# FoX attention of a hybrid decoder layer: plain fp32 on array tiles, 32x32 transposes on VectorE

## The chip, the cores and the metric

The kernel runs on one core of a Trainium2 chip. The metric is the device time of one execution in microseconds. The engines are named as in the profile: PE is TensorE's matrix multiplication (PEld its weight loads), DVE is VectorE, ACT is ScalarE, POOL is GpSimd, SP is SyncE, which issues most DMAs.

## The reference

One decoder layer on 1024 tokens of width 1024. All products are of float32. `u = rmsnorm(x)` is projected by `w_in` into 8 groups of 1024 columns and the forget gates; HGRN2 heads take four groups, FoX heads (16 of width 64) the other four. Their outputs, gated by SiLU, go through one output projection, are added to `x`, gated again and normalised. What the change touches is the FoX branch:

```python
log_f = log_sigmoid(fz + fb)
F = cumsum(log_f, axis=1).transpose(0, 2, 1)
for blk in range(S // Q):            # blocks of 128 queries
    logits = einsum('bhtd,bhsd->bhts', qb, kb) * scale + F[:, :, q0:q1, None] - F[:, :, None, :q1]
    probs = softmax(where(causal, logits, -inf), axis=-1)
    outs.append(einsum('bhts,bhsd->bhtd', probs, vb))
```

## The kernel before

Four stages follow each other: the norm of the input, eight HGRN heads, 16 FoX heads in eight pairs (a pair fills 128 partitions with two heads of 64), and the output projection with gate and norm.

Dense projections are made from two float32r parts of each operand (hi is the rounded value, lo the rest) in three matmuls, hi x hi, hi x lo and lo x hi, all on the full 128x128 array with 512 moving columns. They are jobs of a class `Ahead`: while a head's own steps wait for each other, `ahead.fill(columns)` issues about so many moving columns of the next projections (`FOX_FILL` holds the numbers), `ahead.until(mark)` issues jobs until a projection is done, and `ahead.flush()` issues small transposes that were put off. The numbers and the order of the jobs set the order on PE; the other engines follow the order in which a scheduler lists the instructions of the program. All rows of L363 are dense projections inside `Ahead`; each 512-token half of a job writes one of two PSUM buffers `ps` with 24 matmuls and is then read by ACT and DVE.

A FoX head is worked in two chunks of 512 queries (c = 1 first, then c = 0), and `Chunk.mix(following)` interleaves the values of one chunk with the logits and softmax of the next:

- `fox_q`, `fox_k`, `fox_v` read the projections out of PSUM: q and k become float32r parts (`kh`, `kl`; q holds hi in one half of the partitions and lo in the other, POOL copies k to both halves), v is turned to token-major by PE transposes (L485) and split (`vs`).
- `Chunk.softmax(b)`, for each of four blocks of 128 queries: logits as two float32r matmuls per piece of up to 512 keys (L816, L817); DVE adds the key bias and takes the minimum of the negated logits in one instruction (L820), the block's own keys with a causal bias that POOL has added (`fm`, L801); small DVE minima join the pieces (L826); ACT takes exp with the row sum (L827).
- `Chunk.transposed(j)`: PE transposes the probabilities of key block j, 128x128 each (L835), ACT and DVE split them into float32r parts (L844, L845; L838, L839 for the last block).
- `Chunk.mix`: two matmuls per key block add the values (L867, L868) in one PSUM buffer `po`; ACT and DVE add the two halves into the output (L873, L874).
- `norms` makes 1/Z of a head, through DRAM to all partitions; `finish` multiplies the output with 1/Z and with the gate on POOL and stores it.

The bias rows F come from DRAM (`fd`), one load of 512 KB a head (`biases`).

## Time and profile before

| what | value |
|---|---|
| median of 3 runs | 1362.05 us (1361.67 to 1363.15) |
| span of the profiled execution | 1361.6 us, mean granted PE clock 0.993 |
| PE busy | 1324.1 us, 97% of the span, 8756 matmul records |
| DVE, ACT, POOL busy | 802.6, 552.6, 373.7 us |
| first logits to last values of FoX | 549.7 to 1081.9 us |
| DMA | 100.93 MB, mean 74 GB/s |

The profiled execution's span is within 0.5 us of the median of the runs. A busy share counts from an instruction's start to its modelled end; consecutive matmuls overlap, so the pace of PE is read from the starts. Rows of groups give line, engine, operation, output <- inputs, shape and count, then busy time and the mean of one in ns, then the idle time of the engine ahead of them and what ended it. Matmul rows name the used part of the array (128*128, 128*32) and the moving operand. A plain float32 matmul appears as two records.

### The profile page before, as it was taken

How to read it: one execution, taken by the hardware profiler on the slowest of the kernel's cores; microseconds unless marked ns; L12 is line 12 of the kernel's file. 1: busy time of each engine (PE TensorE's matmuls, PEld its weight loads, DVE VectorE, ACT ScalarE, POOL GpSimd, SP SyncE). 2: the span in 40 equal slices, each digit the busy share in tenths (PEclk: the TensorE clock that was granted, in tenths of full speed). 3: DMA queues.
4: the chain of work that ended last, by engine and by line, in shares of the span. 5: the costliest groups of instructions: out<-in, count | busy, mean ns of one | idle time of the engine just before them, and what ended most of it. 6: DMA issues, size and time to landing. Idle time of an engine off the chain costs nothing.

```text
span 1361.6 us, 22260 instructions
## 1 busy us (share of the span) xinstructions
PE 1324.1 (97%) x8756; PEld 1116.9 (82%) x8756; DVE 802.6 (59%) x1976; ACT 552.6 (41%) x1128; POOL 373.7 (27%) x352
## 2 busy tenths in 40 slices
PE   6899999999999999999999999999999999999996
PEld 4787888888888878888888888888888888888895
DVE  6746575656746576576566666666666843333465
ACT  5413122221312233565555555555565711222455
POOL 3613123112211122344333333333342210101232
PEclk9999999999999999999999999999999999999998
DMA  7411111101101012112121112111123163212312
GB/s 282 144 45 63 48 38 58 63 17 63 48 32 63 19 47 80 47 56 70 55 71 55 56 55 70 54 55 55 70 84 118 63 240 108 85 47 70 132 63 78
DMA packets 35080, 100.93 MB, mean 74 GB/s; under 512 B 5008, under 2 KB 7312, under 8 KB 34976
## 3 DMA queue, kind: packets, MB, share of 16 engines
q1 hardware_dynamic: 34832, 98.99, 20.8%
q8 instruction: 69, 1.13, 0.3%
q0 software_dynamic: 144, 0.52, 0.1%
q14 instruction: 35, 0.29, 0.1%
HBM read 82.59 MB, written 16.91 MB: 73 GB/s over the span
## 4 chain that ended last, share of the span: by engine, by line
PE 87%; DVE 7%; ACT 4%; issue 1%; DMA 1%; SPq 0%; POOL 0%; DVEq 0%; ACTq 0%; POOLq 0%
PE ps L363 47%; PE pt L835 5%; PE ps L105 5%; PE ps L103 5%; PE ps L104 4%; PE po L868 3%; PE po L867 3%; PE lg L816 2%; PE lg L817 2%; PE ps L569 1%; PE gps L105 1%; PE gps L104 1%; PE gps L103 1%; DVE x L279 1%; PE po L712 1%
## 5 line engine op out<-in xcount | busy, mean ns | idle before, releaser
L363 PE MATMUL ps<-uhi,whi 128*128 128x512 f32 x896 | 355.9, 397 | 0.3 <-DVE q L451 0.3
L363 PE MATMUL ps<-ulo,whi 128*128 128x512 f32 x896 | 355.5, 397 | 0.0
L363 PE MATMUL ps<-uhi,wlo 128*128 128x512 f32 x896 | 354.6, 396 | 0.0
L88 POOL TENSOR_TENSOR wlo<-wf,whi 128x1024 fp32r<-128x1024 f32 x59 | 145.3, 2463 | 377.4 <-ACT whi L87 370.8
L363 PEld LDWEIGHTS ps<-uhi,whi 128*128 128x128 f32 x896 | 168.4, 188 | 31.5 <-PE ps L363 0.7
L363 PEld LDWEIGHTS ps<-ulo,whi 128*128 128x128 f32 x896 | 168.5, 188 | 30.4
L363 PEld LDWEIGHTS ps<-uhi,wlo 128*128 128x128 f32 x896 | 168.5, 188 | 30.4
L87 ACT CAST whi<-wf 128x1024 fp32r<-128x1024 f32 (+1 forms) x77 | 79.8, 1038 | 168.7 <-PE ps L104 90.4
L827 ACT ACTIVATE pr<-pr,mx 128x1024 f32<-128x1024 f32 (+7 forms) x128 | 99.6, 778 | 101.3 <-DVE mx L826 94.8
L845 DVE TENSOR_TENSOR pl<-pt,ph 128x512 fp32r<-128x512 f32 (+2 forms) x160 | 94.7, 607 | 75.9 <-ACT ph L844 74.6
L801 POOL TENSOR_TENSOR fm<-fbc,cst 128x128 f32<-128x128 f32 x128 | 59.0, 462 | 251.1 <-DVE mx L826 129.4
L844 ACT CAST ph<-pt 128x512 fp32r<-128x512 f32 (+2 forms) x160 | 79.8, 520 | 70.7 <-PE pt L835 60.1
L105 PE MATMUL ps<-yhi,wlo 128*128 128x512 f32 x256 | 99.6, 389 | 0.0
L103 PE MATMUL ps<-yhi,whi 128*128 128x512 f32 x256 | 99.6, 389 | 0.0
L104 PE MATMUL ps<-ylo,whi 128*128 128x512 f32 x256 | 99.6, 389 | 0.0
L820 DVE CUSTOM_DVE_ANT_0 pr<-lg,fbc 128x512 f32<-128x512 f32 (+3 forms) x176 | 82.0, 490 | 15.5 <-PE lg L817 15.2
L835 PE MATMUL pt<-cst,pr 128*128 128x128 f32 x576 | 89.3, 272 | 1.1 <-ACT pr L827 0.9
L835 PEld LDWEIGHTS pt<-cst,pr 128*128 128x128 f32 x576 | 71.4, 140 | 19.6 <-ACT pr L827 2.2
L816 PE MATMUL lg<-kh,q 128*128 128x512 f32 x192 | 74.7, 389 | 0.0
L817 PE MATMUL lg<-kl,q 128*128 128x512 f32 x192 | 64.1, 341 | 0.0
L867 PE MATMUL po<-ph,vs 128*128 128x512 f32 (+2 forms) x160 | 57.8, 361 | 0.1
L868 PE MATMUL po<-pl,vs 128*128 128x512 f32 (+2 forms) x160 | 57.9, 362 | 0.0
(214 smaller groups left out, 2498.3 us busy)
## 6 DMA issues: line engine op xcount, KB each, us to landing
wf<-in_w_in_dram SPq DMA_DIRECT2D x64, 512.0 KB
fbc<-fd SPq DMA_DIRECT2D x16, 512.0 KB
yf<-yd SPq DMA_DIRECT2D x16, 512.0 KB
wf<-in_w_out_dram SPq DMA_DIRECT2D x16, 512.0 KB
x<-in_xT_dram SPq DMA_DIRECT2D x8, 512.0 KB
pled<-pleo SPq DMA_DIRECT2D x16, 256.0 KB
xr<-in_xT_dram SPq DMA_DIRECT2D x16, 256.0 KB
yd<-sg SPq DMA_DIRECT2D x8, 512.0 KB
```

Of the source, the lines that this page charges most:

```text
L88: pin(lo_engine.tensor_tensor(out=lo, in0=src, in1=hi, op=ALU.subtract))
L103: pin(mm(ps, whi, uhi, start=i == 0, stop=False))
L104: pin(mm(ps, whi, ulo, start=False, stop=False))
L105: pin(mm(ps, wlo, uhi, start=False, stop=i == n - 1))
L363: pe(mm(ps, x, y, start=i == j == 0, stop=i == n - 1 and j == 2))
L816: pe(mm(ps[:, :w], tq, kh[:, s0 : s0 + w], start=True, stop=False))
L817: pe(mm(ps[:, :w], tq, kl[:, s0 : s0 + w], start=False, stop=True))
L827: nc.scalar.activation(pr, pr, AF.Exp, bias=mx[:, 0:1], scale=-1.0, accum_out=zs[:, b : b + 1])
L835: pe(nc.tensor.transpose(pt[:, b * P : (b + 1) * P], self.probs[b][:, j * P : (j + 1) * P], ident))
L845: nc.vector.tensor_tensor(out=pl, in0=pt[:, c0:], in1=ph, op=ALU.subtract)
L867: pe(mm(po[:, c0:], vs[:, j], ph, start=j == 0, stop=False))
L868: pe(mm(po[:, c0:], vs[:, j], pl, start=False, stop=j == nj - 1))
```

## The change

FoX is computed in plain float32 instead of float32r parts, on parts of the array.

- The keys are cut into groups of 32, and groups with an even and with an odd number are kept apart. A row of 128 partitions now holds 64 queries twice: four strips of 32 partitions, two strips of queries by two parities of key groups. `logits(b)` computes two such rows m = 2b + 1 and 2b, each of 64 queries against m + 1 groups of each parity: eight matmuls on array tiles of 64x32 (two row halves, four column strips), N = 32(m + 1) moving columns, into a pair of PSUM banks (L804). q and k are therefore held on both partition halves.
- DVE adds bias and takes the minimum for each m (L816), after POOL has added the causal bias to the last group of the row (`own`, L789; each `own(m - 2)` follows the reading of row m, which uses the same bias tile). `softmax()` of a whole chunk then joins the minima of the two parities (L828, L829), and for each m ACT takes exp with the sum (L836) and DVE transposes all 32x32 blocks of the row (L837) into `probs`. No split follows.
- `values()` multiplies on 64x64 tiles (L848): 64 keys of a group pair in a row half, even and odd pairs in the two column halves, 4 matmuls of up to 256 columns each for two pairs. They are all issued together, after the logits of the following chunk.
- The PSUM pools become two logits buffers of two banks and one buffer `po` of two banks, which the small transposes share. The projections of the next pair come in the order v, q, k, gate. `FOX_FILL` holds one number per pair, used twice a chunk.
- F is stored to DRAM by parity in two DMAs, and its rows come back in four loads a head. The loads of the HGRN outputs for the output projection go into other buffers that are free at that time.

The core of the diff:

```diff
-FOX_FILL = (
-    (1660, 3670, 8820, 2130, 2400),
...
+FOX_FILL = (9200, 12300, 12300, 12300, 12300, 12300, 9200, 4000)
...
-    causal = np.where(r[None, :] > r[:, None], np.float32(BIG), np.float32(0.0)).astype(np.float32)
+    query, key = 32 * (r // 64) + r % 32, 32 * (r // 32 % 2)
+    causal = np.where(key[:, None] + np.arange(32)[None, :] > query[:, None], np.float32(BIG), np.float32(0.0)).astype(np.float32)
...
-    fd = dram.tile([16, S], F32, name="fd")
+    fd = dram.tile([16, 2, CH], F32, name="fd")
...
-            tiles += [T_FQ + p + 1, T_FK + p + 1] + ([T_FG + p] if 0 < p < PAIRS_F - 2 else []) + [T_FV + p + 1]
+            tiles += [T_FV + p + 1, T_FQ + p + 1, T_FK + p + 1] + ([T_FG + p] if 0 < p < PAIRS_F - 2 else [])
...
     def fox_q(p):
-        q = q_t[p] = [fi.tile([P, S], F32R, name="q", tag="q", bufs=4) for _ in range(2)]
+        q = q_t[p] = [fi.tile([P, CH], F32, name="q", tag="q", bufs=4) for _ in range(2)]
...
     def fox_k(p):
-        kh = kh_t[p] = [fp.tile([P, S], F32R, name="kh", tag="kh", bufs=3) for _ in range(2)]
+        k = k_t[p] = [fp.tile([P, S], F32, name="k", tag="k", bufs=3) for _ in range(2)]
...
-                nc.scalar.copy(kh[i][hi, sl], ps[hi])
-                nc.vector.tensor_tensor(out=kl[i][hi, sl], in0=ps[hi], in1=kh[i][hi, sl], op=ALU.subtract)
-                for kk in (kh, kl):
-                    nc.gpsimd.tensor_scalar(
-                        out=kk[i][lo, sl], in0=kk[i][hi, sl], scalar1=1.0, scalar2=1.0, op0=ALU.mult, op1=ALU.mult
-                    )
+                nc.scalar.copy(k[i][half[0], sl], ps[half[i]])
+                nc.vector.tensor_copy(out=k[i][half[1], sl], in_=ps[half[i]])
...
-        vs = v_t[p] = [fp.tile([P, FB, P], F32R, name="vs", tag="vs", bufs=3) for _ in range(2)]
+        v = v_t[p] = fp.tile([P, 2 * FB, P], F32, name="v")
...
-                    nc.scalar.copy(dst[:, :, hi], pv[:, :, hi])
-                    nc.vector.tensor_tensor(out=dst[:, :, lo], in0=pv[:, :, hi], in1=dst[:, :, hi], op=ALU.subtract)
+                    pe(nc.tensor.transpose(pt[:, 0, b * P : (b + 1) * P], vt[:, b * P : (b + 1) * P], ident))
+                dst = v[:, 8 * c : 8 * c + 8].rearrange("p (b r) d -> p b r d", r=2)
+                for r in range(2):
+                    src = pt[half[r], 0].rearrange("p (b d) -> p b d", d=P)
+                    nc.scalar.copy(dst[half[0], :, r], src)
+                    nc.vector.tensor_copy(out=dst[half[1], :, r], in_=src)
...
-        lg = st.enter_context(tc.tile_pool(name="lg", bufs=3, space=PSUM, reuse_waits="tile"))
-        tr = st.enter_context(tc.tile_pool(name="tr", bufs=2, space=PSUM, reuse_waits="tile"))
+        lg = st.enter_context(tc.tile_pool(name="lg", bufs=2, space=PSUM, reuse_waits="tile"))
...
-                    fbc[self.head] = fp.tile([P, S], F32, name="fbc")
-                    nc.sync.dma_start(out=fbc[self.head], in_=fd[self.head : self.head + 1, :].to_broadcast([P, S]))
-            def diagonals(self):
...
-                    nc.gpsimd.tensor_tensor(out=fm, in0=fbc[self.head][:, b * P : (b + 1) * P], in1=causal, op=ALU.add)
-            def softmax(self, b):
...
-                    pe(mm(ps[:, :w], tq, kh[:, s0 : s0 + w], start=True, stop=False))
-                    pe(mm(ps[:, :w], tq, kl[:, s0 : s0 + w], start=False, stop=True))
...
-                            nc.vector.tensor_tensor_reduce(
-                                out=pr[:, e0:e1], in0=ps[:, e0 - s0 : e1 - s0], in1=bias, scale=1.0, scalar=BIG,
-                                op0=ALU.add, op1=ALU.min, accum_out=mx[:, parts : parts + 1],
...
-                for j in range(1, parts):
-                    nc.vector.tensor_tensor(out=mx[:, 0:1], in0=mx[:, 0:1], in1=mx[:, j : j + 1], op=ALU.min)
-                nc.scalar.activation(pr, pr, AF.Exp, bias=mx[:, 0:1], scale=-1.0, accum_out=zs[:, b : b + 1])
...
-            def transposed(self, j):
...
-                for b in range(first, 4):
-                    pe(nc.tensor.transpose(pt[:, b * P : (b + 1) * P], self.probs[b][:, j * P : (j + 1) * P], ident))
...
-                nc.scalar.copy(ph, pt[:, c0:])
-                nc.vector.tensor_tensor(out=pl, in0=pt[:, c0:], in1=ph, op=ALU.subtract)
...
-            def mix(self, following):
...
-                ahead.fill(FOX_FILL[self.p][0 if self.c == 0 else 1 if self.i else 2])
-                nxt = self.transposed(0)
...
-                        nxt = self.transposed(j + 1)
-                    if blocks and j % (nj // 4) == 0:
-                        following.softmax(blocks.pop(0))
-                    ahead.fill(FOX_FILL[self.p][3 + self.c])
...
-                    pe(mm(po[:, c0:], vs[:, j], ph, start=j == 0, stop=False))
-                    pe(mm(po[:, c0:], vs[:, j], pl, start=False, stop=j == nj - 1))
...
+                    fb2 = fp.tile([P, 2, CH], F32, name="fb")
+                    fbc[self.head] = [fb2[:, r].rearrange("p (t k) -> p t k", k=32) for r in range(2)]
+                    z_t[self.head] = fp.tile([P, 2 * FB], F32, name="zs")
+                    for j in range(4):
+                        row = fd[self.head : self.head + 1, j % 2 : j % 2 + 1]
+                        nc.sync.dma_start(out=fb2[32 * j : 32 * j + 32], in_=row.to_broadcast([32, 2, CH]))
+                    self.own(2 * FB - 1)
+                    self.own(2 * FB - 2)
+            def own(self, m):
+                t = fbc[self.head][m % 2][:, m]
+                nc.gpsimd.tensor_tensor(out=t, in0=t, in1=causal, op=ALU.add)
+            def logits(self, b):
+                q, k = (t[self.p][self.i] for t in (q_t, k_t))
+                if b % 4 == 3:
+                    self.x = fp.tile([P, 64 * self.c + 36, 32], F32, name=f"x{self.c}", bufs=1)
+                    self.mx = fp.tile([P, 8], F32, name="mx")
+                    self.xs = {}
+                ps = lg.tile([P, 2, CH], F32, name="lg", tag="lg")
+                ms = (2 * b + 1, 2 * b)
+                for j in range(4):
+                    for m in ms:
+                        rows, n = half[m % 2], m + 1
+                        pe(
+                            mm(
+                                ps[32 * j : 32 * j + 32, m % 2, : 32 * n],
+                                q[rows, 64 * (m // 2) + 32 * (j // 2) :][:, :32],
+                                k[rows].rearrange("p (t a k) -> p t a k", a=2, k=32)[:, :n, j % 2],
+                                start=True,
+                                stop=True,
+                            )
+                        )
+                for m in ms:
+                    n = m + 1
+                    o = sum(x + 1 for x in range(8 * self.c, m))
+                    x = self.xs[m] = self.x[:, o : o + n].rearrange("p t k -> p (t k)")
+                    nc.vector.tensor_tensor_reduce(
+                        out=x, in0=ps[:, m % 2, : 32 * n], in1=fbc[self.head][m % 2][:, :n].rearrange("p t k -> p (t k)"),
+                        scale=1.0, scalar=BIG, op0=ALU.add, op1=ALU.min, accum_out=self.mx[:, m % 8 : m % 8 + 1],
+                    )
+                    if m > 1:
+                        self.own(m - 2)
+            def softmax(self):
+                zs = z_t[self.head]
+                other = fp.tile([P, 8], F32, name="mxo")
+                for j in range(4):
+                    nc.vector.tensor_copy(out=other[32 * (j ^ 1) : 32 * (j ^ 1) + 32], in_=self.mx[32 * j : 32 * j + 32])
+                nc.vector.tensor_tensor(out=other, in0=other, in1=self.mx, op=ALU.min)
+                self.probs = fp.tile([P, 8 * self.c + 8, 8, 32], F32, name=f"pt{self.c}", bufs=1)
+                if self.c == 0:
+                    nc.gpsimd.memset(self.probs[:, 1, 0], 0.0)
+                for m in reversed(range(8 * self.c, 8 * self.c + 8)):
+                    x, g = self.xs[m], m % 8
+                    nc.scalar.activation(x, x, AF.Exp, bias=other[:, g : g + 1], scale=-1.0, accum_out=zs[:, m : m + 1])
+                    nc.vector.transpose(self.probs[:, : m + 1, g], x.rearrange("p (t k) -> p t k", k=32))
+            def values(self):
+                po = av.tile([P, 2, CH], F32, name="po", tag="po")
+                n = 8 * self.c + 8
+                for t in range(n):
+                    first = max(t - 8 * self.c, 0) if t > 1 else 0
+                    for r in range(2):
+                        pe(
+                            mm(
+                                po[half[t % 2], r, 32 * first : 256],
+                                v_t[self.p][half[r], t, half[self.i]],
+                                self.probs[half[r], t, first:].rearrange("p g q -> p (g q)"),
+                                start=t < 2,
+                                stop=t >= n - 2,
+                            )
+                        )
...
+            def mix(self, following):
+                if following:
+                    for b in (3, 2, 1, 0):
+                        following.logits(4 * following.c + b)
+                        if b % 2 == 0:
+                            ahead.fill(FOX_FILL[self.p])
+                    following.softmax()
+                else:
+                    ahead.fill(10000)
+                ahead.flush()
+                self.values()
...
-        for b in reversed(range(4, 8)):
-            chunks[0].softmax(b)
+        for b in (7, 6, 5, 4):
+            chunks[0].logits(b)
             ahead.fill(3560)
+        chunks[0].softmax()
...
-                    ahead.jobs += [fox_q(p + 1), fox_k(p + 1)]
+                    ahead.jobs += [fox_v(p + 1), fox_q(p + 1), fox_k(p + 1)]
                     if 0 < p < PAIRS_F - 2:
                         ahead.jobs.append(fox_gate(p))
-                    ahead.jobs.append(fox_v(p + 1))
...
-                for x in ((fi, "q", 4), (fi, "q", 4), (fp, "kh", 3), (fp, "kl", 3)):
-                    y_load(*x)
+                y_load(fp, "pt1", 1, 4)
```

What this does to the order of instructions. PE in a middle pair, one key block of a chunk before (`pt` are transposed probabilities, `lg` logits, `ps` a dense projection, `po` values):

```order
L835 MATMUL pt_7325<-cst_291,pr4_7258 128x128
...
L835 MATMUL pt_7335<-cst_291,pr4_7258 128x128
...
L816 MATMUL lg_7346<-kh_6318,q_6145 128x512
L817 MATMUL lg_7346<-kl_6320,q_6145 128x512
L363 MATMUL ps_7310<-uhi_283,wlo_7092 128x512
...
L363 MATMUL ps_7310<-ulo_288,whi_7091 128x512
L867 MATMUL po_7334<-ph_7330,vs_6695 128x512
L868 MATMUL po_7334<-pl_7331,vs_6695 128x512
L835 MATMUL pt_7361<-cst_291,pr4_7258 128x128
```

Between a transpose and the values that use it stand another key block's transposes, a logits block of the next chunk and dense matmuls; every step is on the full array. PE in the same place now, from the last logits block of one chunk to the first of the next:

```order
L804 MATMUL lg_6388<-k_5864,q_5651 32x320
L804 MATMUL lg_6388<-k_5864,q_5651 32x288
...
L356 MATMUL ps_6373<-ulo_276,whi_6139 128x512
...
L356 MATMUL ps_6436<-uhi_275,whi_6234 128x512
L848 MATMUL po_6461<-pt0_6246,v_5459 64x256 x4
L848 MATMUL po_6461<-pt0_6246,v_5459 64x192 x2
...
L848 MATMUL po_6461<-pt0_6246,v_5459 64x32 x2
L804 MATMUL lg_6491<-k_5864,q_5651 32x256
L804 MATMUL lg_6491<-k_5864,q_5651 32x224
...
L804 MATMUL lg_6504<-k_5864,q_5651 32x192
```

The transposes of probabilities are gone from PE, the values of a chunk stand in one piece, and the next logits follow them directly; behind each pair of logits blocks stand about 24 dense matmuls.

DVE before, in the softmax and transposes of a chunk (`pl` is the lo part of transposed probabilities):

```order
L845 TENSOR_TENSOR pl_7331<-pt_7325,ph_7330 128x512
L845 TENSOR_TENSOR pl_7341<-pt_7335,ph_7340 128x512
L820 ISA pr3_7344,mx_7345<-lg_7346,fbc_6901 128x384
L820 ISA mx_7345 128x1
L820 ISA pr3_7344,mx_7345<-lg_7346,fm_7285 128x128
L820 ISA mx_7345 128x1
L826 TENSOR_TENSOR mx_7345<-mx_7345 128x1
L845 TENSOR_TENSOR pl_7367<-pt_7361,ph_7366 128x512
L438 SCALAR_TENSOR_TENSOR sg_7303<-sg_7303,ps_7310 128x512
```

DVE now, from the last logits of chunk `x1_6309` to the first of the next (`mx` are minima, `mxo` the joined ones, `pt1` the transposed probabilities):

```order
L816 ISA x1_6309,mx_6310<-lg_6388,fb_6100 128x288
L816 ISA mx_6310 128x1
L828 COPY mxo_6438<-mx_6310 32x8 x4
L829 TENSOR_TENSOR mxo_6438<-mxo_6438,mx_6310 128x8
L837 STREAM_TRANSPOSE pt1_6444<-x1_6309 128x16x32
L837 STREAM_TRANSPOSE pt1_6444<-x1_6309 128x15x32
...
L837 STREAM_TRANSPOSE pt1_6444<-x1_6309 128x9x32
L860 TENSOR_TENSOR o_6099<-po_6461,avt_6478 64x2x8x32
L816 ISA x0_6489,mx_6490<-lg_6491,fb_6100 128x256
```

A logits row of the next chunk, which before stood among the splits, now stands behind all eight transposes of the chunk and the output sum (`o`) of the chunk before.

PE at the boundary from pair 6 to pair 7:

```order
L356 MATMUL ps_10273<-uhi_289,wlo_9968 128x512
L804 MATMUL lg_10304<-k_10176,q_9963 32x512
...
L804 MATMUL lg_10317<-k_10176,q_9963 32x448
...
L804 MATMUL lg_10330<-k_10176,q_9963 32x384
...
L804 MATMUL lg_10343<-k_10176,q_9963 32x320
...
L886 MATMUL pz_10379<-cst_291,zs_9746 16x128
L848 MATMUL po_10388<-pt0_10203,v_9052 64x256 x4
...
L804 MATMUL lg_10427<-k_10176,q_9963 32x256
```

Here all four logits blocks of a chunk follow each other without dense matmuls between them; the same holds at the boundary from pair 0 to pair 1.

136 lines of the change are left out of this document (43 added, 93 removed).

## Prediction

> **What bounds the kernel now.** I read the page's busy times first, then the stage that the change rewrites, then the chain of waits inside it, then single stretches of the timeline. The busy times:
>
> ```profile
> PE 1324.1 (97%) x8756; PEld 1116.9 (82%) x8756; DVE 802.6 (59%) x1976; ACT 552.6 (41%) x1128; POOL 373.7 (27%) x352
> ```
>
> The tensor engine works 97% of the span, so a microsecond matters if it is taken from that engine or makes it wait. The FoX stage lies between the first logits and the last values, and its row among the windows is:
>
> ```profile
> core 0: us, PE busy (x) PEld busy (x) DVE busy (x) ACT busy (x) POOL busy (x), PEclk, DMA share, GB/s
> 549.70:1081.90 532.20, 531.01 (x2799) 444.43 (x2798) 340.15 (x1134) 303.68 (x652) 190.82 (x224) 1.00 0.19 66
> ```
>
> In 532.2 us the tensor engine is idle for 1.2 us, while VectorE has 340 us of work and ScalarE 304 us. The clock is 1.00 throughout, so the throttle plays no part. The chain of waits within 549 to 1082 us (533 us) says what that tensor time is:
>
> ```profile
> by line: PE ps L363 57.7%; PE pt L835 11.8%; PE po L868 6.5%; PE po L867 6.5%; PE lg L816 6.3%; PE lg L817 6.3%; PE pt L485 1.3%; ACT pr L827 1.0%; ACT yhi L87 0.4%; DVE mx L826 0.4%; DVE pr L820 0.3%; PE pt L883 0.3%; issue 0.2%; ACT whi L
> ```
>
> 57.7% is the dense projections (L363), which the change keeps, 3264 matmuls in the whole program before and after. The work of the heads is L835 (transposes of the probabilities), L867 and L868 (values) and L816 and L817 (logits): 11.8 + 6.5 + 6.5 + 6.3 + 6.3 = 37.4%, or 199 us. The 2.3% on ScalarE, VectorE and issue (12 us) are short waits of the same steps. The timeline gives the pace:
>
> ```profile
> 657.42 0.40 PE L363 MATMUL ps<-ulo,whi 128*128 128x512 f32 x1
> 657.66 1.04 PE L835 MATMUL pt<-cst,pr 128*128 128x128 f32 x8
> 658.45 0.48 PE L816 MATMUL lg<-kh,q 128*128 128x512 f32 x1
> 658.76 0.39 PE L817 MATMUL lg<-kl,q 128*128 128x512 f32 x1
> 659.00 0.39 PE L363 MATMUL ps<-uhi,wlo 128*128 128x512 f32 x1
> ```
>
> A dense matmul of 512 float32r columns starts 0.23 us after the one before it (0.447 ns a column). The eight transposes last from 657.66 to 658.45, and the first logits matmul behind them takes 0.08 us more than 0.23: 0.87 us for eight, 0.109 us each, 576 x 0.109 = 63 us, which is the chain's 11.8%.
>
> **What the change removes.** From the tensor engine go the 199 us above. With them I take off 10 of the 12 us of short waits, since they stand at steps that go (a transpose waiting for its exponential); the lowest value is 0, if the waits return one for one.
>
> **What it adds on the tensor engine.** Plain fp32 on tiles has its nearest rows in the HGRN stage, which already uses 128x32 and 128x64 tiles in fp32 (x64 records are 32 matmuls, two each):
>
> ```profile
> 102.94 0.39 PE L363 MATMUL ps<-uhi,wlo 128*128 128x512 f32 x1
> 103.25 0.89 PE L569 MATMUL ps<-x,k 128*32 128x48 f32 x64
> 104.07 0.50 PE L363 MATMUL ps<-uhi,whi 128*128 128x512 f32 x1
> 104.41 0.40 PE L363 MATMUL ps<-ulo,whi 128*128 128x512 f32 x1
> ...
> 118.44 0.39 PE L363 MATMUL ps<-ulo,whi 128*128 128x512 f32 x1
> 118.76 1.15 PE L660 MATMUL pd<-x,k 128*64 128x64 f32 x16
> 119.83 0.50 PE L363 MATMUL ps<-uhi,wlo 128*128 128x512 f32 x1
> 120.17 0.39 PE L363 MATMUL ps<-uhi,whi 128*128 128x512 f32 x1
> ...
> 301.42 0.39 PE L710 MATMUL po<-v,st 128*128 128x128 f32 x2
> 301.64 0.39 PE L712 MATMUL po<-state,x 128*128 128x128 f32 x2
> ```
>
> The last two rows give the pace without overlap: two records of 128 columns take 0.22 us, so an fp32 matmul costs 1.74 ns a column, four times a float32r one. The first group shows the overlap: 64 records of 48 columns would take 2.67 us one after the other (0.87 ns each column), and they take 0.82 us from 103.25 to 104.07, entry and exit included. Four tiles side by side really run four at a time (0.67 us). Row halves do not occur in this trace. Bounds for two row halves: they overlap fully (eight logits tiles and four value tiles at a time), or not at all, which doubles both terms below. I take the full overlap, because the nearest row shows independent tiles at their full number.
>
> Logits: block b is one wave of eight matmuls, the longest with 64(b+1) columns; over b = 0..7 that is 2304 columns x 1.74 ns = 4.0 us a head, 64 us for 16 heads. Values: per head 12 waves of four, the longest of each 5 x 256 + 192 + 128 + 64 columns in the later half of the queries and 256 + 192 + 128 + 64 in the earlier, again 2304 columns, 64 us. Together 128 us.
>
> Each change of tile shape costs time. Into the 128x32 block the start-to-start time is 0.31 us instead of 0.23; the block takes 0.82 instead of 0.67; the first dense matmul behind it 0.34 instead of 0.23: 0.34 us there and back. The 128x64 block, where only one tile is used, gives 0.09 + 0.18 + 0.11 = 0.38 us. In the new order the tensor engine goes from full to tiled 67 times: 67 x 0.35 = 23 us. From values straight to logits it goes 28 times; nothing shows that, it lies between 0 and 0.35 us, I take 0.2, 6 us. Both ends are 0 and 10 us.
>
> Without new waits: 199 + 10 - 128 - 29 = 52 us less.
>
> **What it moves to the other engines.** VectorE and ScalarE, from the groups of the FoX stage:
>
> ```profile
> L845 DVE TENSOR_TENSOR pl<-pt,ph 128x512 fp32r<-128x512 f32 (+2 forms) x160 | 94.7, 607 | 75.9 <-ACT ph L844 74.6
> L820 DVE CUSTOM_DVE_ANT_0 pr<-lg,fbc 128x512 f32<-128x512 f32 (+3 forms) x176 | 82.0, 490 | 15.5 <-PE lg L817 15.2
> ...
> L826 DVE TENSOR_TENSOR mx<-mx 128x1 f32<-128x1 f32 x176 | 51.6, 293 | 3.2
> L820 DVE CUSTOM_DVE_ANT_0 pr<-lg,fm 128x128 f32<-128x128 f32 x128 | 36.4, 284 | 4.8 <-PE lg L817 4.5
> L820 DVE CUSTOM_DVE_ANT_0 pr<-lg,fbc 128x512 f32<-128x512 f32 x48 | 32.7, 682 | 3.1 <-PE lg L817 3.1
> L820 DVE DVE_READ_ACCUMULATOR2_ANT mx<- 128x1 f32 x304 | 24.9, 82 | 0.0
> L874 DVE TENSOR_TENSOR o<-po,avt 64x512 f32<-64x512 f32 x31 | 21.4, 689 | 43.9 <-ACT avt L873 34.1 <-issue 9.7
> ```
>
> ```profile
> L827 ACT ACTIVATE pr<-pr,mx 128x1024 f32<-128x1024 f32 (+7 forms) x128 | 99.6, 778 | 101.3 <-DVE mx L826 94.8
> L844 ACT CAST ph<-pt 128x512 fp32r<-128x512 f32 (+2 forms) x160 | 79.8, 520 | 70.7 <-PE pt L835 60.1
> ...
> L87 ACT CAST whi<-wf 128x1024 fp32r<-128x1024 f32 x28 | 29.3, 1046 | 2.6 <-issue 1.2 <-PE ps L363 0.9
> L827 ACT ACTIVATION_READ_ACCUMULATOR pr<-pr,mx 128x1 f32 x128 | 23.9, 187 | 0.0
> L827 ACT ACTIVATE pr<-pr,mx 128x1024 f32<-128x1024 f32 x16 | 18.4, 1153 | 5.1 <-DVE mx L826 4.9
> L827 ACT ACTIVATE pr<-pr,mx 128x128 f32<-128x128 f32 x16 | 6.4, 403 | 6.1 <-DVE mx L820 6.0
> L465 ACT CAST kh<-ps 64x512 fp32r<-64x512 f32 x28 | 16.2, 579 | 6.4 <-PE ps L363 5.2 <-DVE kl L466 0.8
> ```
>
> VectorE loses the splits of L845 (95 us) and the minima of L826 (52). Its logits pass goes from 304 instructions to 256 over 69632 columns a partition; the L820 rows of one shape give 0.15 us + 1.04 ns a column, the read-out 0.08: 132 us against 82 + 36 + 25 = 143. New are 256 transposes over the same 69632 columns. No row shows one. At the pace of the other VectorE rows (0.15 us + 1.04 ns) they are 112 us; at a quarter of that pace 329 us; below 0 is impossible. I take 112, since every fp32 VectorE row here runs at about 1.04 ns a column. With 32 x 5 small instructions (at most 0.29 each, the row of L826, 46 us) VectorE comes to 340 - 95 - 52 - 11 + 112 + 46 = 340 us of a stage of some 500.
>
> ScalarE loses the casts of L844 (80 us). The exponentials double in number: 0.30 us + 0.84 ns a column + 0.19 for the read-out, 256 x 0.49 + 58 = 183 us against 100 + 24. With them it has 304 - 80 + 59 = 283 us. Neither engine is full, but their loop is long, and that is where I expect the tensor engine to wait.
>
> The Trainium skill, in "VectorE: DVE Perf Modes", section "The three transpose paths", gives 311 ns on VectorE for a 128x128 block of bf16, in 32x32 pieces, and its rules advise TensorE for a 128x128 transpose where a PSUM destination is acceptable. Estimated from that figure the 544 blocks cost 169 us instead of 112, the eight of a long chunk (below) 7.8 us instead of 4.6; that loop would grow by some 1.6 us and the time by 19 us, to 1350. No run here shows a VectorE transpose, and my sum stays with the rows.
>
> The loop: in a half of the queries ("chunk") VectorE reads the last logits, forms the minima, ScalarE runs eight exponentials, VectorE transposes them in step, and the next chunk's logits stand behind those transposes in VectorE's order. They must be read before the third logits block of that chunk has a PSUM buffer. From a long chunk (8 to 16 key groups) to a short one: two reads 1.1, minima 1.0 (at most 5 x 0.29), exponentials 8 x 0.49 + 3200 x 0.84 ns = 6.6, a weight cast 1.05 and two evacuations 1.2 (L465's 0.58 each) on ScalarE in between, last transpose 0.45, output sum 0.7, two reads 0.95: 13.0 us. The tensor engine meanwhile has 48 dense matmuls (11.0), short values 1.1, two logits blocks 0.8 and four switches 0.7: 13.6 us. So it is covered, by 0.6 us. From a short chunk to a long one 11 us stand against 16.
>
> Where cover is missing: pair 0 has 36 dense matmuls per chunk, 8.2 instead of 11.0 us: 13.0 against 10.8, 2 us in all, since there some reads stand between the transposes. At the boundaries 0 to 1 and 6 to 7 four logits blocks follow each other with no dense work: k's copies (0.58 on ScalarE by L465, then 0.69 on VectorE as in L874) 1.5 us, and the third and fourth block wait for reads, 2 us: 3.5 us each, 7 in all. Pair 7 has 16 dense matmuls per chunk: 13.0 less the evacuations and with two reads ahead of the transposes, some 10 us, against 6.3, twice, and 1 once, and the first of them behind the boundary: 10 us. Middle pairs 0.5 each. Together 22 us.
>
> Costed at nothing: the copies of q, k and v go to the same two engines in pieces of the same or half the width; they lie beside 5.5 us of dense work per PSUM buffer and cost their own 0.7 us each where that is gone (counted at the boundaries). GpSimd and the queues:
>
> ```profile
> L801 POOL TENSOR_TENSOR fm<-fbc,cst 128x128 f32<-128x128 f32 x128 | 59.0, 462 | 251.1 <-DVE mx L826 129.4
> ...
> fbc<-fd SPq DMA_DIRECT2D x16, 512.0 KB
> ```
>
> The causal sums go from 128 of 128 columns to 256 of 32. Even at 0.46 us each that would be 118 us, beside 500; each now stands between two reads of VectorE, covered by the read of the other row half, and can queue behind a weight split on GpSimd; VectorE's next read and the PSUM evacuations behind it then wait, inside the 5.5 us of dense work between two pairs of logits blocks. GpSimd loses k's duplication. The bias rows come as four loads a head instead of one of 512 KB, two chunks ahead; F is written in two pieces before the stage. If that cover failed, one transfer a head is a few microseconds.
>
> **The sum.** 1361.6 - 199 - 10 + 128 + 29 + 22 = 1331.6 us; the profiled execution stands 0.4 us under the median of 1362.05, so I say 1331.
>
> **Rivals.** First, no new waits: that the tensor engine idles only 1.2 us now speaks for it, the counted loops against; 1331 - 22 = 1309 us. Second, the softmax loop decides everywhere: its cover in the middle pairs is 0.6 us of 13.6, and 2 us more on the loop (a slower transpose, a longer minimum) gives 1.4 us in 12 middle steps, and with longer ones at pairs 0 and 7 some 25 us: 1356 us. Against it: ScalarE and VectorE stay under 70% busy. Third, on the other side: the row halves do not overlap. Then 128 us become 256 and the time is 1459 us; it decides against the change once the two halves run under 1.6 at a time instead of 2 (256 / 1.6 = 160, 32 us over 128). For it: no row shows row tiles. Against: column tiles reach their full number. The Trainium skill, in "TensorE: Matmul & The Clock Gate", part "Packing small matmuls — row/col tiling", reports 3.07 times for four row tiles and 10.6 times for sixteen, which is against this rival; no run here shows it. Fourth, VectorE transposes at a quarter of the pace: 329 us instead of 112 give VectorE 557 us, more than the stage has; the stage becomes VectorE's, 25 us longer than before, 1387 us. No row speaks for it.
>
> **How the numbers follow.** Forecast 0.55 (1320 to 1345), no waits 0.12, loop everywhere 0.17 (1345 to 1366), row halves 0.09, slow transposes 0.05, the rest 0.02. The range 1307 to 1364 leaves out the last three and the end of the second rival. A measurement tells 0.2%, 2.7 us, from no change: faster 0.80, within 0.04, slower 0.16.
>
> **What would show it.** Right: between the first logits and the last values about 500 us, no transposes of probabilities on the tensor engine, a 512-column logits wave of about 0.9 us, values of a long chunk 2.9 us, 0.35 us per excursion, idle time of the tensor engine about 22 us, mostly in pair 7 and at two boundaries. Wrong: logits waves of 1.8 us or longer (row halves), VectorE transposes of 512 columns far over 0.69 us, or idle time before the third logits block in every pair (loop).

## The result, and the profile after

The changed kernel takes 1411.4 us (median of 4 runs, 1411.1 to 1411.8) against 1362.6 of the kernel before: a ratio of 1.036 [1.034, 1.037], slower by 49 us where 31 us less were forecast. The profiled execution spans 1409.3 us. Its page says:

```profile
PE 1300.6 (92%) x10996; PEld 1032.5 (73%) x10996; DVE 800.7 (57%) x1940; ACT 496.2 (35%) x1192; POOL 337.8 (24%) x432
```

TensorE fell from 97% to 92% and no other engine is near full: it waits. The windows view, first for the FoX stage (first logits to last values) and what follows it, and for one middle pair:

```profile
547.43:1116.58 569.15, 498.88 (x5008) 354.25 (x5007) 332.94 (x1092) 241.28 (x703) 159.44 (x308) 0.93 0.18 59
735.00:809.90 74.90, 67.53 (x652) 49.09 (x651) 42.60 (x139) 31.38 (x90) 22.09 (x40) 0.93 0.18 58
1116.58:1409.30 292.72, 276.19 (x1385) 234.45 (x1381) 133.09 (x176) 97.13 (x150) 45.50 (x29) 0.97 0.31 102
```

The columns are the stretch, its length, the busy time of PE, PEld, DVE, ACT and POOL with counts, the granted clock, and the DMA share and rate. The stage takes 569.2 us where 532.2 stood before, TensorE is idle for 70 us of it, and the clock, 1.00 before, is 0.93. The same view of before, for a pair at the same point of the program:

```profile
719.10:790.00 70.90, 70.90 (x372) 59.37 (x371) 43.10 (x143) 38.61 (x82) 26.47 (x30) 1.00 0.17 60
```

A middle pair takes 74.9 us instead of 70.9; of these TensorE is idle for 7.4. What it waited for within the stage, from the chain of waits by engine (us in total, times, longest):

```profile
PE pt L479 <- ACT vt L474: 25.6, 8, 5.6
PE po L848 <- DVE v L484: 19.1, 7, 2.8
PE lg L804 <- DVE mx L816: 11.9, 10, 2.5
PE po L848 <- DVE zt L891: 4.9, 3, 2.3
PE lg L804 <- DVE k L463: 4.5, 2, 2.3
PE pt L479 <- DVE zt L891: 2.9, 2, 1.4
PE pz L886 <- DVE o L860: 1.3, 1, 1.3
```

The two largest are not the softmax loop. They belong to v of the next pair: its second half is evacuated by ScalarE (vt, L474), transposed by TensorE (L479) into the tile that the values use too (one PSUM buffer, `av` with the tag "po"), copied out (L483, L484), and only then may the values (L848) write there. The timeline of one such place, TensorE first, then ScalarE, then VectorE and GpSimd a little earlier:

```profile
648.07 1.12 PE L479 MATMUL pt<-cst,vt 128*128 128x128 f32 x4 [5.59 <-ACT vt L474]
652.01 5.11 PE L848 MATMUL po<-pt,v 64*64 64x256 f32 x64 [2.82 <-DVE v L484]
...
642.07 0.51 ACT L836 ACTIVATE x<-x,mxo 128x256 f32<-128x256 f32 x1 [6.04 <-DVE mxo L829]
646.36 1.03 ACT L80 CAST whi<-wf 128x1024 fp32r<-128x1024 f32 x1
647.42 0.60 ACT L474 ACTIVATE vt<-ps 128x512 f32<-128x512 f32 x1
649.22 0.58 ACT L483 COPY v<-pt 64x512 f32<-64x512 f32 x1 [1.21 <-PE pt L479]
...
635.29 2.39 POOL L904 TENSOR_TENSOR o<-o,rz 128x1024 f32<-128x1024 f32 x1 [1.26 <-DVE o L860]
637.92 0.29 DVE L816 CUSTOM_DVE_ANT_0 x<-lg,fb 128x128 f32<-128x128 f32 x1 [2.07 <-POOL fb L789]
638.05 2.40 POOL L906 TENSOR_TENSOR o<-o,sg 128x1024 f32<-128x1024 f32 x1
640.69 0.23 DVE L816 CUSTOM_DVE_ANT_0 x<-lg,fb 128x64 f32<-128x64 f32 x1 [2.29 <-POOL fb L789]
```

Read from below: GpSimd multiplies a finished output by one over the row sums and by the gate (L904, L906, 2.4 us each); the causal additions (L789) stand among them, and VectorE's logits pass waits 2.07 and 2.29 us for them. So the exponentials start only at 642.07. In ScalarE's order vt stands behind all eight of them and a weight cast, and is done at 648.0. TensorE waits 5.59 us, transposes for 1.12, and waits 2.82 more until four copies have taken turns on the buffer. Then the values take 5.11 us, though the same 64 records (32 matmuls) take 3.03 elsewhere (run 10 below): after the wait the clock is at half.

```profile
720.00:722.00 2.00, 0.00 (x0) 0.00 (x0) 0.99 (x4) 1.98 (x8) 0.21 (x1) 0.77 0.00 0
722.00:724.00 2.00, 1.11 (x4) 0.71 (x4) 0.00 (x0) 0.80 (x2) 2.00 (x1) 0.50 0.00 0
724.00:726.00 2.00, 0.00 (x0) 0.00 (x0) 1.20 (x2) 0.70 (x2) 0.55 (x3) 0.50 0.43 88
726.00:732.00 6.00, 5.68 (x72) 4.14 (x80) 0.17 (x1) 0.06 (x1) 0.00 (x0) 0.56 0.15 58
```

These windows are of the next pair. TensorE stops at 718.8; 2.3 us later the clock goes to 0.50 and stays there for 10.2 us, through the values. Summed over the stage, from the clock records and the matmuls under them, TensorE works 54 us at half clock, which is 27 us lost. Waits and halved clock together are 97 us.

### The profile page after: what moved, and what is told of

Same layout as the page of the kernel before. It is cut to its first block, busy times and chain, and to the rows that moved or that the text cites. A ratio compares the mean times of both kernels' runs of the same rounds, so it can differ in the third digit from the quotient of the medians.

```text
span 1409.3 us, 26890 instructions
## 1 busy us (share of the span) xinstructions
PE 1300.6 (92%) x10996; PEld 1032.5 (73%) x10996; DVE 800.7 (57%) x1940; ACT 496.2 (35%) x1192; POOL 337.8 (24%) x432
## 4 chain that ended last, share of the span: by engine, by line
PE 71%; DVE 11%; ACT 6%; issue 5%; POOL 4%; DMA 2%; SPq 1%; DVEq 0%; ACTq 0%; POOLq 0%
PE ps L356 39%; PE po L848 5%; PE ps L98 4%; PE ps L97 4%; PE ps L96 4%; PE lg L804 3%; DVE x L816 2%; ACT x L836 2%; PE ps L562 1%; PE gps L98 1%; PE gps L97 1%; PE gps L96 1%; POOL wlo L81 1%; POOL o L906 1%; DVE x L272 1%
## 5 line engine op out<-in xcount | busy, mean ns | idle before, releaser
L81 POOL TENSOR_TENSOR wlo<-wf,whi 128x1024 fp32r<-128x1024 f32 x59 | 145.0, 2457 | 490.2 <-ACT whi L80 484.2
L836 ACT ACTIVATE x<-x,mxo 128x512 f32<-128x512 f32 (+15 forms) x256 | 130.3, 511 | 104.2 <-DVE mxo L829 104.2
L816 DVE CUSTOM_DVE_ANT_0 x<-lg,fb 128x512 f32<-128x512 f32 (+15 forms) x256 | 102.4, 436 | 55.6 <-POOL fb L789 36.4
L837 DVE STREAM_TRANSPOSE pt<-x 128x512 f32<-128x512 f32 (+15 forms) x256 | 112.1, 456 | 26.9 <-ACT x L836 23.0
L789 POOL TENSOR_TENSOR fb<-fb,cst 128x32 f32<-128x32 f32 x256 | 62.8, 253 | 222.0 <-DVE mx L816 207.5
L848 PE MATMUL po<-pt,v 64*64 64x256 f32 (+7 forms) x1536 | 84.8, 368 | 24.1 <-DVE v L484 19.1
L848 PEld LDWEIGHTS po<-pt,v 64*64 64x64 f32 x1536 | 64.1, 153 | 52.1 <-issue 29.4
L96 PE MATMUL ps<-yhi,whi 128*128 128x512 f32 x256 | 99.9, 391 | 0.0
L804 PE MATMUL lg<-k,q 64*32 64x352 f32 (+15 forms) x2048 | 82.2, 410 | 16.5 <-DVE mx L816 11.9
L804 PEld LDWEIGHTS lg<-k,q 64*32 64x32 f32 x2048 | 32.4, 107 | 50.6 <-issue 24.2
L97 PEld LDWEIGHTS ps<-ylo,whi 128*128 128x128 f32 x256 | 48.5, 189 | 14.0 <-DVE ylo L81 3.9
L96 PEld LDWEIGHTS ps<-yhi,whi 128*128 128x128 f32 x256 | 48.4, 189 | 10.1
L98 PEld LDWEIGHTS ps<-yhi,wlo 128*128 128x128 f32 x256 | 48.5, 189 | 9.9
```

What stands on the lines that cost most here:

```text
L81: pin(lo_engine.tensor_tensor(out=lo, in0=src, in1=hi, op=ALU.subtract))
L96: pin(mm(ps, whi, uhi, start=i == 0, stop=False))
L97: pin(mm(ps, whi, ulo, start=False, stop=False))
L98: pin(mm(ps, wlo, uhi, start=False, stop=i == n - 1))
L789: nc.gpsimd.tensor_tensor(out=t, in0=t, in1=causal, op=ALU.add)
L804: mm(ps[32 * j : 32 * j + 32, m % 2, : 32 * n], q[rows, 64 * (m // 2) + 32 * (j // 2) :][:, :32], k[rows].rearrange("p (t a k) -> p t a k" ...
```

## The experiments

Times are medians; all were timed in turn with the kernel before on the same chip, and the ratios are to it. Unless said otherwise a gain is counted from the 1411.4 us of the changed kernel.

**1. The additions on VectorE.**

```diff
-  nc.gpsimd.tensor_tensor(out=t, in0=t, in1=causal, op=ALU.add)
+  nc.vector.tensor_tensor(out=t, in0=t, in1=causal, op=ALU.add)
```

> The 256 causal additions go from GpSimd to VectorE, nothing else. Theory A (a queue on GpSimd): once per pair two additions stand behind a weight split and the two output multiplies, 2.4 us each, VectorE's logits reads wait 5 us for them, the exponentials start 5 us late, the evacuation of v^T behind them too, and TensorE waits for it. Then the 25.6 us that TensorE waits for v^T fall below 8, the 19 us that the values wait for the v copies stay, and the time falls from 1411 to about 1380 us (1370 to 1392). Rival B (VectorE's and ScalarE's loop is too long by itself): VectorE gets 256 x 0.19 = 49 us more, the loop grows, TensorE's waits stay or grow: 1411 to 1430 us.

Measured: 1409.8 us, ratio 1.034 [1.033, 1.036]: 1.6 us less with overlapping intervals, and 22.2 of the 25.6 us for v^T stay. As I had put it theory A falls. Rival B's waits "stay or grow", and TensorE's idle time in the stage did stay (69.7 us after 70.3), so this run alone doesn't exclude it; but the additions keep VectorE busy for 66 us in the stage without making that idle time longer, and run 9 speaks against it. The timeline of VectorE, and of GpSimd beside it:

```profile
706.50 1.16 DVE L789 TENSOR_TENSOR fb<-fb,cst 128x32 f32<-128x32 f32 x1
708.29 1.83 DVE L789 TENSOR_TENSOR fb<-fb,cst 128x32 f32<-128x32 f32 x2
710.41 2.05 DVE L789 TENSOR_TENSOR fb<-fb,cst 128x32 f32<-128x32 f32 x1
712.78 0.30 DVE L789 TENSOR_TENSOR fb<-fb,cst 128x32 f32<-128x32 f32 x2
...
705.21 2.40 POOL L81 TENSOR_TENSOR wlo<-wf,whi 128x1024 fp32r<-128x1024 f32 x1 [2.60 <-ACT whi L80]
707.57 2.40 POOL L904 TENSOR_TENSOR o<-o,rz 128x1024 f32<-128x1024 f32 x1
710.04 2.37 POOL L906 TENSOR_TENSOR o<-o,sg 128x1024 f32<-128x1024 f32 x1
```

An addition of 32 columns takes 0.15 us when GpSimd is still (two in 0.30), and 1.16 to 2.05 us while GpSimd runs a 1024-column operation: each ends as that operation ends (707.6, 710.0, 712.4). The additions were held up by GpSimd's long operations, the weight split and the two multiplies, in either place; moving them away from GpSimd's queue changed who was blocked, and TensorE waited as long. The Trainium skill says so in "SBUF — State Buffer", section "Who interferes with whom": a VectorE instruction with two SBUF inputs contends with a GpSimd instruction that reads SBUF, and the one that is second blocks for the other's whole length. The run agrees, with these numbers. The logits pass, which reads one input from PSUM, is not stretched there (0.39 us for 224 columns at 707.69).

**2. The values ahead of v's transposes.** GpSimd stays as it is.

```diff
                 else:
                     ahead.fill(10000)
-                ahead.flush()
+                    ahead.flush()
                 self.values()
...
                 ahead.fill()
+                ahead.flush()
                 finish(p, False)
```

> In each step the values are issued before the transposes of the next pair's v, which move behind the next chunk's first logits blocks and six dense matmuls; GpSimd is as before. Theory A (the values stand behind transposes that they don't need, and share a PSUM buffer with them): the waits of TensorE for v^T (25.6 us) and for the v copies and row sums (27 us) go nearly all, and with the idle stretches the clock stays at 1.00, so that long chunks' values take 2.96 us everywhere (13 us in five pairs): 1350 to 1365 us. Rival B (the softmax loop is too long by itself): the wait reappears before the next logits or values, and the time stays above 1395 us. Rival C (the clock falls because of plain fp32 on tiles, not because of idling): 0.50 stretches stay in every pair although TensorE doesn't idle, about 1370 us or more.

Measured: 1400.3 us, ratio 1.028 [1.026, 1.029]: 11 us less where 46 to 61 were expected. The wait for v^T went, as expected (25.6 to 4.0 us), and the long values take 2.96 us in every pair; of the half-clock stretches in the middle pairs (five of 10.2 us) four of 3.4 us are left, each at the 2.8 us wait in the table below. That speaks against rival C; run 7 settles it. But other waits took its place:

```profile
PE pz L886 <- DVE o L860: 16.4, 3, 7.6
PE pz L886 <- DVE v L484: 14.1, 5, 2.8
PE po L848 <- DVE v L484: 13.7, 7, 2.5
PE lg L804 <- DVE mx L816: 9.0, 8, 2.5
```

The first three are one thing: row sums (pz), v's transposes and values take turns on one PSUM buffer, and whoever is second waits for the other's evacuation. The time lies in rival B's range (above 1395), and B named the values as well as the logits. The logits' wait is 9 us, no more than before; that the others belong to the buffer and not to a long loop is shown only by runs 5 and 6.

**3. Both of these edits.**

> Both edits: the additions on VectorE and the values before the transposes of v. Theory A: the order alone takes the values out of the chain, so the additions add little: within 8 us of the order alone, either sign, 1345 to 1365 us. Rival B: VectorE's longer loop shows, 1400 us or more. If the two waits were independent causes, the savings would add up: about 1320 to 1330 us.

Measured: 1392.2 us, ratio 1.022 [1.020, 1.024], 8 us under the order alone. No theory's number fits: A counted on the order to do nearly everything, B on VectorE to slow it down; and the savings (11 and 2 us alone, 19 together) don't add up either. The buffer was still there.

**4. Copies dealt by PSUM half.** In the changed kernel both engines read the same 64 PSUM partitions in turn; here each is given its own.

```diff
-  for r in range(2):
-      src = pt[half[r], 0] ...
-      nc.scalar.copy(dst[half[0], :, r], src)
-      nc.vector.tensor_copy(out=dst[half[1], :, r], in_=src)
+  for h in range(2):
+      nc.scalar.copy(dst[half[h], :, 0], src[0])
+      nc.vector.tensor_copy(out=dst[half[h], :, 1], in_=src[1])
```

> Only the four copies that follow each block of v transposes are dealt otherwise: ScalarE takes both copies of the lower 64 PSUM partitions, VectorE both of the upper 64, so that they needn't take turns on one half. Theory A: the chain of four copies (0.58, 0.69, 0.58, 0.69 us in turn, 2.8 us) becomes two in parallel, 1.4 us, in front of the values of about seven steps: 8 to 11 us less, about 1402 us. Rival (the wait for v^T decides and the copies are only seen by accident): under 3 us.

Measured: 1408.3 us, ratio 1.033 [1.032, 1.035]: 3 us less, on the edge of the rival, and the intervals overlap. The wait of the values for the copies barely moved (19.1 to 18.6 us). The timeline says why:

```profile
648.78 0.58 ACT L483 COPY v<-pt 64x512 f32<-64x512 f32 x1 [1.20 <-PE pt L479]
649.39 0.69 DVE L484 COPY v<-pt 64x512 f32<-64x512 f32 x1 [3.00 <-ACT v L483]
650.12 0.58 ACT L483 COPY v<-pt 64x512 f32<-64x512 f32 x1 [0.76 <-DVE v L484]
650.73 0.69 DVE L484 COPY v<-pt 64x512 f32<-64x512 f32 x1 [0.64 <-ACT v L483]
```

The four copies still follow each other, each waiting for the other engine's, 2.6 us in all. Other partitions did not make them run in parallel, so what parallel copies would be worth is not shown, for the theory or for the rival. What keeps them in turn stays open.

**5. Another PSUM buffer, the old order.** Row sums and v's transposes write into the two buffers of the logits.

```diff
-  pt = av.tile([P, 2, CH], F32, name="pt", tag="po")
+  pt = lg.tile([P, 2, CH], F32, name="pt", tag="lg")
...
-  pz = av.tile([P, 2, CH], F32, name="pz", tag="po")
+  pz = lg.tile([P, 2, CH], F32, name="pz", tag="lg")
```

> The changed kernel, only that the transposes of v and of the row sums write into the logits' two PSUM buffers and no longer into the single buffer of the values; the order is the old one. Theory A, as the order alone corrected it (one PSUM buffer for three uses; whoever comes second waits for the evacuation of the first): the waits of the values for the v copies and row sums (19 + 5 us) and two small ones (4 us) go, the wait for v^T on ScalarE (25.6 us) stays, the clock is halved in fewer or shorter stretches: 1370 to 1388 us. Rival B (the loop of VectorE and ScalarE is the bound, the buffer only where it shows): the same idle time comes back in front of the logits: 1400 us or more.

Measured: 1378.7 us, ratio 1.012 [1.010, 1.014]: 33 us less, as theory A said. All waits of the values are gone from the trace, 21.2 us for v^T stay, and the time lost to the half clock falls from 27 to 13 us.

**6. Order and buffer.**

> The values ahead of the transposes of v, and these in the logits' PSUM buffers. Theory A: of the order alone (1400 us) 16 + 14 us of row sums waiting for the buffer, 14 us of values waiting for v copies and 5 us of small ones go: 1345 to 1362 us, and the clock is 1.00 in the middle pairs. Rival B: VectorE reads the logits no earlier, idle time appears in front of logits blocks, 1385 us or more.

Measured: 1369.4 us, ratio 1.005 [1.003, 1.007]: 42 us less, 7 us above theory A's range, far under rival B. From pair 2 to pair 5 nothing of v or the row sums is waited for any more except for 0.7 us a pair, and the clock is 1.00 there. What is left in the stage is mostly VectorE; the second row stands behind the stage:

```profile
PE lg L804 <- DVE mx L816: 19.4, 11, 4.7
PE ps L96 <- DVE h L990: 5.5, 1, 5.5
PE pt L479 <- DVE mx L816: 4.6, 5, 1.8
PE lg L804 <- DVE k L463: 4.5, 2, 2.3
PE pt L479 <- ACT vt L474: 4.0, 2, 3.8
```

**7. The multiplies on VectorE as well.**

```diff
-  nc.gpsimd.tensor_tensor(out=o, in0=o, in1=rz_t.pop(p), op=ALU.mult)
+  nc.vector.tensor_tensor(out=o, in0=o, in1=rz_t.pop(p), op=ALU.mult)
...
-  nc.gpsimd.tensor_tensor(out=o, in0=o, in1=sg_t[p], op=ALU.mult)
+  nc.vector.tensor_tensor(out=o, in0=o, in1=sg_t[p], op=ALU.mult)
```

> As the run with both edits, and the two multiplies a pair that finish the outputs (1024 columns, 2.4 us each on GpSimd) go to VectorE. In the kernel whose additions ran on VectorE, a 32-column addition took 0.15 us, but 1.16 to 2.05 us while such a multiply ran on GpSimd: the multiplies hold up the additions on either engine. Theory A: VectorE waits some 5 us less a pair and works 2.4 us more; where this still reaches TensorE it gives 3 to 10 us: 1340 to 1358 us. Rival B: VectorE's loop is the bound: slower by 5 us or more.

Measured: 1352.0 us, ratio 0.993 [0.991, 0.994]: 0.7% under the kernel before, and 17 us better than the run ahead of it, where 3 to 10 were expected. The profiled executions of the two runs differ by 22 us: 12 lie in the stage and 8 behind it, where this run doesn't have the wait of 5.5 us (L96) that nobody had in view. The windows of a middle pair and of the stage:

```profile
714.90:780.10 65.20, 64.33 (x651) 47.03 (x652) 45.46 (x140) 31.29 (x91) 19.44 (x39) 1.00 0.20 66
547.26:1061.42 514.16, 483.70 (x5008) 344.69 (x5007) 351.07 (x1106) 240.93 (x703) 136.71 (x294) 0.97 0.20 65
```

The pair takes 65.2 us at clock 1.00, with 0.9 us idle, where the changed kernel takes 74.9 and the kernel before 70.9. The 30 us of idle time that the stage still has lie mostly at the first pair, the two boundaries and the last pair; the 0.97 comes from the clock at half in and behind such waits.

**8. All copies dealt by half (q, k and v), on top.** The edit of run 4, and its like for k and q.

> As the run before it, and the copies of q, k and v out of PSUM are dealt so that ScalarE reads the lower 64 partitions and VectorE the upper 64 at the same time, in place of turns on each half. Alone this gave 3 us for v. Theory A: the waits of logits for k at two boundaries (4.5 us) halve, dense groups get their PSUM buffer earlier: 2 to 8 us less, 1335 to 1355 us. Rival: nothing waits for them any more but at the boundaries, 0 to 2 us.

Measured: 1354.2 us, ratio 0.995 [0.993, 0.996], 2 us more, with overlapping intervals. As in run 4 the copies still take turns in the trace (VectorE waits 28.6 us in the stage for ScalarE's copies of k, and 29.4 in run 7), and the logits' wait for k at the two boundaries is 5.5 us instead of 4.5. So neither theory was put to the test.

**9. The multiplies alone.** The edit of run 7 in the changed kernel and nothing else.

> The changed kernel with one edit: the two output multiplies a pair on VectorE in place of GpSimd. On top of the order and the buffers this edit gave 17 us. If that was a cause of its own (VectorE's reads held up on a GpSimd that is busy), it gives 12 to 20 us here too: about 1393 us, and the waits for v^T fall by half. Rival: while the values stand behind the transposes of v, those wait for the evacuations all the same: under 6 us, 1405 us or more.

Measured: 1387.0 us, ratio 1.018 [1.017, 1.020]: 24 us less. VectorE waits 4.1 us for the additions in front of its logits pass instead of 36.4. The wait for v^T is 12.5 us instead of 25.6, and the 19 us of the values behind the copies are as before. So GpSimd's long operations are a cause of their own, more than expected. The three edits alone give 11, 33 and 24 us, together 59.

**10. One row half left out.** In the kernel of run 7 the value matmuls of r = 1 are not issued and the output takes r = 0 twice: half of the value matmuls, 384 of 768 (two records each), are missing.

```diff
-  for r in range(2):
+  for r in range(1):
       pe(mm(po[half[t % 2], r, 32 * first : 256], ...
```

> The kernel of 1352 us with half of the value matmuls left out: the row half r = 1 isn't computed, and r = 0 is added to itself. Theory A (two row halves run side by side at full speed, as the prediction assumed): the values of a long chunk stay near the 2.96 us that both halves take together (2.8 to 3.0), and the time stays within 6 us of 1352. Rival (halves share the array in part): the long chunk falls to 1.5 to 2.4 us, and the time by 9 to 34 us.

Measured: 1354.3 us, ratio 0.995 [0.993, 0.996], no gain. The values of a long chunk with both halves, and with one:

```profile
675.04 3.03 PE L848 MATMUL po<-pt,v 64*64 64x256 f32 x64
678.00 1.83 PE L804 MATMUL lg<-k,q 64*32 64x512 f32 x32
```

```profile
676.98 3.03 PE L848 MATMUL po<-pt,v 64*64 64x256 f32 x32
679.94 1.83 PE L804 MATMUL lg<-k,q 64*32 64x512 f32 x32
```

From start to start 2.96 us both times, with 64 records and with 32: the second row half costs nothing.

**11. Jobs in the order q, k, v.** On top of run 7, with the loads of the weights in the same order; it is meant for the boundaries from pair 0 to 1 and 6 to 7.

```diff
-  ahead.jobs += [fox_v(p + 1), fox_q(p + 1), fox_k(p + 1)]
+  ahead.jobs += [fox_q(p + 1), fox_k(p + 1), fox_v(p + 1)]
```

> As the fastest run so far (1352 us: values first, own buffers, multiplies on VectorE), and the dense jobs of the next pair run in the order q, k, v in place of v, q, k, so that k is ready long before the boundary and dense matmuls are left for the places between the logits blocks at the boundaries from pair 0 to 1 and from 6 to 7. Theory A: there TensorE now waits 2.3 us for k's copies and 0.9 to 4.7 us before logits blocks that follow each other, and the clock is halved behind it: twice about 9 us, 1332 to 1342 us. Rival (the loop of VectorE and ScalarE is too long at these boundaries, whatever the order): under 5 us, 1347 us or more.

Measured: 1351.4 us, ratio 0.992 [0.991, 0.994], no gain. The wait for k is gone and one for v stands in its place:

```profile
PE pt L479 <- ACT vt L474: 11.0, 3, 3.8
PE lg L804 <- DVE mx L816: 9.7, 8, 2.6
PE lg L804 <- DVE v L484: 3.8, 1, 3.8
```

**12. And v's last transposes later.** The flush that run 2 added ahead of `finish` is kept for the last pair alone, so that at a boundary these transposes go into the next dense group.

```diff
                 ahead.fill()
-                ahead.flush()
+                if p == PAIRS_F - 1:
+                    ahead.flush()
                 finish(p, False)
```

> As the run with the order q, k, v (1351 us), and at the two boundaries the last transposes of v are no longer issued right behind the short chunk's values but in the next dense group. In that run TensorE waited there 3.6 us for v^T on ScalarE, then 3.8 and 1.8 us before the logits for the copies of v, with the clock halved behind it. Theory A (an early place in TensorE's order makes the wait): these 13 us go but for 2 to 3 us of the loop: 1339 to 1345 us. Rival (the softmax loop of the boundary step is too long whatever TensorE is given there): the wait moves to the logits, under 4 us: 1347 us or more.

Measured: 1341.3 us (median of 5, 1336.7 to 1343.1), ratio 0.983 [0.982, 0.985], the fastest of all and as theory A said. The wait for v^T is 3.8 us, that for v's copies 0.6, and VectorE at the logits 10.4. In the stage TensorE is idle for 23 us and loses 9 to the half clock.

## Why the prediction was wrong, point by point

**The step that failed is the list of new waits, "Together 22 us".** Idle time and halved clock came to 97 us in the stage. The sum gave the stage 502 us; 28 dense matmuls (6.5 us) moved behind it, which leaves 496 to compare with 569, a miss of 73; the waits are 75 of it and the other terms of the stage together are within 2 us. Behind the stage 6.5 us more were lost than the moved matmuls explain: 3.1 us are waits of TensorE for a split on VectorE (L81) that the kernel before does not have there, and a half-clock stretch of 3.4 us follows them; the rest stays open. Three sentences that it rests on did not hold for the changed kernel:

- "Costed at nothing: the copies of q, k and v". I priced them as busy time beside dense work and never asked what stands behind v's transposes on TensorE. It was the values, in the same single PSUM buffer. Run 5 shows it: with another buffer and nothing else, 33 us less. Run 2 shows that the order alone doesn't repair it.
- "The causal sums": I let them queue behind a weight split "inside the 5.5 us of dense work". They met the split and two multiplies, some 7 us in a row. Run 9 puts the multiplies at 24 us, and run 1 shows that leaving GpSimd's queue doesn't help the additions, because VectorE is then held up instead.
- "The throttle plays no part": that holds for a TensorE that never stops. In every wait of 3.5 us or more in the stage of the changed kernel the clock went to half, so waits cost more than their length. Run 7 has the same tile work at clock 1.00 from 632 to 963 us, in pairs 2 to 5 and most of pair 1: idling is the cause, not plain fp32.

**What held.** Logits and values take 4.5 and 4.2 us a head where nothing is waited for, 139 us. In run 7 a tiled stretch starts 0.32 us behind the last dense matmul instead of 0.23 (674.72 to 675.04), and the first dense matmul behind one takes 0.34 (679.77 to 680.11): 0.20 us a switch, 13 us for 67, some 153 in all. "128 + 29" was 4 too much, because a switch costs less than 0.35. The "10 of the 12 us of short waits" had the right size for a wrong reason: TensorE idled only 1.2 us in that stage, so they weren't waits of its own. In a middle pair of the kernel before, the 192 dense matmuls take 45.1 us from start to start and would take 43.9 at the pace of 16 in 3.66 us; these 1.2 us a pair, 10 in all, lie mostly behind transposes, where the first dense matmul takes 0.32 instead of 0.23. Row halves overlap fully: run 10, the third rival out. VectorE's transposes, from the groups of the stage:

```profile
L837 DVE STREAM_TRANSPOSE pt<-x 128x512 f32<-128x512 f32 (+15 forms) x256 | 112.1, 456 | 26.9 <-ACT x L836 23.0
L816 DVE CUSTOM_DVE_ANT_0 x<-lg,fb 128x512 f32<-128x512 f32 (+15 forms) x256 | 102.4, 436 | 55.6 <-POOL fb L789 36.4 <-PE lg L804 17.5
```

112.1 us against 112: the estimate from the pace of the other VectorE rows was right, though to the microsecond by chance (256 times the mean of 456 ns is 117, before the overlaps of neighbours are taken off). The fourth rival is out, and so is the 169 us estimate beside it. The idle column of the second row (36.4 us waiting for GpSimd) is the row that I should have foreseen. The softmax loop is covered in the middle pairs, as counted: 0.9 us idle in run 7 against 0.5. A middle pair by the sum is 70.9 - 24.9 - 1.3 + 16 + 3.6 + 0.5 = 64.8 us; run 7 has 65.2. So the gain exists, and the changed kernel gave it back, and more, mostly at one place a pair. In run 12 TensorE idles 23 us in the stage, where the sum had 22; since the last pair has 3 of them and not 10, that match is luck.

**The rivals.** None of the four named this place. The second, the loop everywhere at 1356, was nearest in kind but put the wait at the logits, where 12 us were seen. No bound of the range allowed for one wait causing the next and a halved clock behind both.

## What to carry to other kernels

When a step moves to other tiles, list for each PSUM buffer all its users and the instruction that each use puts behind it on TensorE, not only the engine time of the copies: a transposition that nobody needs soon can stand ahead of work that is ready. Repair such a place by buffer and order together (11 and 33 us alone, 42 together here), then ask what starts the chain (here the multiplies on GpSimd, 24 us alone). Price a TensorE wait of about 3 us or more at more than its length, since the clock that is lost is paid by the matmuls that follow.

## What the runs showed of the hardware

- The clock falls to 0.50 some 2 to 4 us after TensorE stops, and the half-clock stretch lasts a multiple of 3.4 us, 10.2 in the middle pairs of the changed kernel: 64 records of values take 5.0 to 5.7 us from start to start instead of 2.96. The Trainium skill, "TensorE: Matmul & The Clock Gate", section "HAM oscillation — how this bites in real kernels", has the rule that TensorE should have no idle gap over some 3.4 us; gaps of 3.55 and 5.59 us agree. In run 2 gaps of 2.8 us were enough in four of five pairs, and in run 7 two of 1.1 and 1.2 us, 0.5 us apart, were followed by 3.4 us at half clock, so the limit can't be taken as safe.
- A VectorE addition that reads two SBUF tiles was held up until GpSimd's 1024-column operation ended: 0.15 us became up to 2.05 us (run 1). That VectorE holds up GpSimd in the same way, no run here shows.
- Two row halves times two column halves of plain fp32 run fully side by side: 2.96 us for 64 records or 32, where the 1664 columns of one tile in four, at the 1.74 ns of the kernel before, are 2.9.
- An fp32 transposition in 32x32 blocks on VectorE takes 0.31 us for 128x128 and 0.71 for 128x512, which is 0.18 us and 1.04 ns a column.
